# A hybrid decoder trunk: first sums of squares on TensorE, and a gate's reciprocal as exp(-ln)

## The chip, the cores and the metric

The kernel runs on one core of one Trainium2 chip. The metric is device microseconds of one launch, the median of several runs. Four compute engines work beside each other, each through its own queue of instructions in order: TensorE (PE; its weight loads are shown apart as PEld), VectorE (DVE), ScalarE (ACT) and GpSimd (POOL). SyncE (SP) only issues transfers here. An instruction waits at the head of its queue until the engines and transfers that it depends on have signalled, and everything behind it on that engine waits too.

## The reference, cut to what matters

Two layers, 512 tokens, 1024 features, all in float32. Each layer normalises its input, multiplies by one wide matrix, runs three groups of heads, and then an MLP:

```python
def rmsnorm(x, g):
    y = x * lax.rsqrt(jnp.mean(x * x, axis=-1, keepdims=True) + EPS)
    return y * g

h = rmsnorm(x, g_mix[l])
(cq, ckv, kr, aq, ak, av, qi, ki, wi, rq, rk, rv, rg) = jnp.split(h @ w_in[l], split_at, axis=-1)
...                      # three groups of heads: latent, sparse (top 128 keys), retention
ret = head_groupnorm(ret, g_ret[l])
o_c = jax.nn.silu(rg) * ret
x = x + jnp.concatenate([o_a, o_b, o_c], axis=-1) @ w_out[l]
hf = rmsnorm(x, g_mlp[l])
x = x + jnp.square(jax.nn.relu(hf @ w_ff1[l])) @ w_ff2[l]
```

`silu(rg)` is rg / (1 + exp(-rg)).

## The kernel before, in words

Activations stand with features on the 128 partitions and the 512 tokens along the free dimension, so the input is eight tiles `x[0]` to `x[7]` of 128x512. Every float32 product is made of three: a value is split into a rounded part (`hi`, `wh`) and the rest (`lo`, `wl`), and `mm3` adds hi·hi, hi·lo and lo·hi. A weight tile of 128 output columns (`win_tile(n)`) is one transfer into a buffer `wr`, two halves rounded by ACT or POOL into `wh` (L187, L189), the rests `wl` by DVE or POOL (L209, L211), and 24 matmuls into one PSUM bank `mm`. The rings are short: four buffers each for `wr`, `wh` and `wl`, three banks each for `mm` and `sc`.

The normalisation is taken out of the product: the matmuls read the bare x times the gain (`make_u`, u), and the factor 1/rms of each token multiplies the result when it leaves PSUM (`scaled`, by `rb`, which holds the factor in every partition; `rtok` holds it with tokens on partitions). So the first products can start before the factor is known, but nothing leaves PSUM until it is.

The factor of the first layer is made at the start: eight squares of x (L618 on POOL, L621 on ACT), seven adds into one tile `ss` (L624 on DVE), four matmuls of `ss` with a column of ones (`stats`, which put 128 tokens on partitions each), logarithm, exponential and one Newton step on 128x4 numbers (`rstd`), and four transposes that spread the result (`bcast`). The letters in `SQP` give the engine of each square: a is ACT, p is POOL.

The first products are, in order, tile 0 (keys; through `rope`), tiles 1 and 7 and 2 as the string `ORDER` lists them (`qi0 rg0 qi1`), and then `tk`, the token tiles, which are 96 matmuls of 328 columns. `rope` needs a transfer that swaps rows, two products with a table (one on POOL, one on DVE) and an add on DVE. After `tk` come the index scores (`sc` matmuls, relu on ACT, weighted sums on DVE), and from there on DVE finds the top 128 keys by rounds of MAX8 and MATCH_REPLACE8, which are set between everything else.

The gate is `rg_tile`, twice per layer: the tile leaves PSUM scaled, DVE clamps and negates it (L846), ACT takes the exponential (L847), POOL adds 1 (L848), DVE takes the reciprocal (L851), POOL multiplies (L852). The result is read much later, by `ret_done`.

What order the instructions take on each engine is settled when the program is built: a list scheduler places them by the order in which the code issues them, their dependencies, and the priorities in `PRI` (through `hp`); `tc.issue_after` holds an instruction back behind another. On the chip the order is fixed. So a change in one place can move instructions in others.

## Time and profile before

| | |
|---|---|
| runs | 1391.5, 1395.73 and 1395.9 us; median 1395.73 |
| the profiled execution's own time | 1398.68 us |
| its span | 1396.9 us |
| PE busy | 1326.8 us, 95% |
| DVE busy | 1103.2 us, 79% |
| ACT busy | 666.2 us, 48% |
| POOL busy | 331.6 us, 24% |
| granted clock of TensorE, mean | 0.976 |

A share of busy time is a mean over stages. How it is read: the span begins with some 40 us in which the first products wait for inputs; then comes a stretch up to about 330 us in which PE and DVE are both nearly full, then the MLP of the first layer in which PE has no gap, and the same again for the second layer. L numbers are lines of the kernel before. A row of a timeline gives the start, how long the engine was busy, the engine, the line, what is written and read, and in brackets how long the engine stood idle before it and what ended that. A granted clock of 1.00 is TensorE's upper level (2.4 GHz) and 0.50 its lower one (1.2 GHz).

### The profile page before, as it was taken

Reading aid. Unit: us, or ns where it says so; the run is one execution under the profiler, and the core shown is the slowest. Engines: PE = TensorE matmul, PEld = TensorE weight load, DVE = VectorE, ACT = ScalarE, POOL = GpSimd, SP = SyncE. Lnnn points to the kernel's source line nnn. Section 1 sums busy time; section 2 is a strip of 40 time slices with the busy share of each in tenths; the row PEclk is TensorE's granted clock in tenths of the full one; section 3 lists DMA queues with packets and bytes.
Section 4 is the critical chain, followed back from the end, with each engine's and each line's share of the span. In section 5 each row is a group of like instructions: output and inputs, shape, how many; then the busy total and the mean of one; then the engine's idle time right before and its main releaser. Section 6 shows DMA issues by size and latency. Waiting matters only on the chain. (4 is left out here: it accounts for less than half of the span.)

```text
span 1396.9 us, 20211 instructions
## 1 busy us (share of the span) xinstructions
PE 1326.8 (95%) x7304; PEld 1102.9 (79%) x7304; DVE 1103.2 (79%) x1843; ACT 666.2 (48%) x1179; POOL 331.6 (24%) x337
## 2 busy tenths in 40 slices
PE   7889988989999999999999999898999999999997
PEld 5767775757788888899988777566778888888997
DVE  6789998887677767788658999878767776777875
ACT  3343443676344344455535345357844444445652
POOL 4446752424100000000034666334240000000000
PEclk9999999999999999999999999999999999999998
DMA  6457522302355554556546671231035555554652
GB/s 218 99 162 183 157 64 70 113 16 63 123 192 171 183 174 154 180 180 215 178 143 188 192 181 52 77 100 46 16 121 163 164 179 178 161 180 151 209 184 78
DMA packets 75780, 197.56 MB, mean 141 GB/s; under 512 B 8960, under 2 KB 13792, under 8 KB 75680
## 3 DMA queue, kind: packets, MB, share of 16 engines
q1 hardware_dynamic: 74528, 195.22, 45.6%
q8 instruction: 58, 0.95, 0.3%
q10 hardware_dynamic: 1152, 1.05, 0.2%
q14 instruction: 42, 0.34, 0.1%
HBM read 155.68 MB, written 20.97 MB: 126 GB/s over the span
## 5 line engine op out<-in xcount | busy, mean ns | idle before, releaser
L141 PE MATMUL mm<-u,wh 128*128 128x512 f32 (+1 forms) x1776 | 561.5, 396 | 1.6 <-DVE u L284 1.2
L141 PEld LDWEIGHTS mm<-u,wh 128*128 128x128 f32 x1776 | 332.7, 190 | 77.4 <-DVE u L284 2.6
L141 PE MATMUL mm<-u,wl 128*128 128x512 f32 (+1 forms) x888 | 351.0, 395 | 3.9 <-DVE wl L209 3.9
L187 ACT ACTIVATE wh<-wr 128x512 fp32r<-128x512 f32 (+2 forms) x247 | 149.8, 611 | 315.8 <-PE mm L141 197.3
L209 DVE TENSOR_TENSOR wl<-wr,wh 128x512 fp32r<-128x512 f32 (+2 forms) x208 | 153.5, 739 | 89.6 <-ACT wh L187 87.3
L211 POOL TENSOR_TENSOR wl<-wr,wh 128x512 fp32r<-128x512 f32 (+2 forms) x80 | 104.7, 1309 | 443.3 <-ACT wh L187 423.7
L141 PEld LDWEIGHTS mm<-u,wl 128*128 128x128 f32 x888 | 168.8, 190 | 43.4 <-DVE wl L209 4.8
L489 DVE TENSOR_TENSOR u<-wr,u 128x1024 fp32r<-128x1024 f32 x54 | 65.8, 1221 | 25.1 <-ACT u L488 24.7
L141 PE MATMUL o<-p,v 128*128 128x512 f32 (+2 forms) x316 | 83.4, 370 | 1.8 <-POOL p L138 1.3
L488 ACT ACTIVATE u<-wr 128x1024 fp32r<-128x1024 f32 x54 | 57.1, 1058 | 53.3 <-PE o L502 14.0
L431 DVE TENSOR_TENSOR sm<-wr 128x512 f32<-128x512 f32 x64 | 44.5, 695 | 36.3 <-DMA wr<-in_wff 36.3
L502 PEld LDWEIGHTS sc<-g,v 128*128 128x128 f32 x576 | 70.3, 188 | 2.9
L502 PE MATMUL sc<-g,v 128*128 128x256 f32 x576 | 71.0, 277 | 0.0
L141 PEld LDWEIGHTS o<-p,v 128*128 128x128 f32 x316 | 52.4, 198 | 12.8 <-DVE p L138 4.1
L419 DVE SCALAR_TENSOR_TENSOR g<-mm,g 128x512 f32<-128x512 f32 x64 | 44.1, 688 | 23.0 <-PE mm L141 22.8
L138 DVE TENSOR_TENSOR p<-pe,p 128x512 fp32r<-128x512 f32 (+2 forms) x78 | 46.5, 623 | 12.0 <-POOL p L189 9.9
L189 POOL TENSOR_SCALAR p<-pe 128x512 fp32r<-128x512 f32 (+1 forms) x46 | 35.1, 767 | 74.2 <-ACT pe L1082 72.6
L735 DVE MATCH_REPLACE8 g<-m,g 128x512 f32<-128x512 f32 (+2 forms) x96 | 51.4, 539 | 0.0
L734 DVE MAX8 m<-g 128x8 f32<-128x256 f32 (+2 forms) x96 | 50.3, 547 | 0.2
L435 ACT ACTIVATE v<-wr 128x1024 fp32r<-128x1024 f32 x32 | 34.1, 1066 | 33.3 <-DVE wr L433 33.1
L189 POOL TENSOR_SCALAR wh<-wr 128x512 fp32r<-128x512 f32 (+3 forms) x41 | 29.8, 726 | 82.9 <-PE mm L141 57.6
L141 PE MATMUL sc<-u,qk 97*128 97x512 f32 (+5 forms) x192 | 46.7, 358 | 2.4 <-ACT pe L1082 2.4
(299 smaller groups left out, 2742.0 us busy)
## 6 DMA issues: line engine op xcount, KB each, us to landing
wr<-in_wff SPq DMA_DIRECT2D x160, 512.0 KB
wr<-in_win SPq DMA_DIRECT2D x37, 512.0 KB
ws<-sm SPq DMA_DIRECT2D x32, 512.0 KB
wr<-ws SPq DMA_DIRECT2D x32, 512.0 KB
tab<-in_tabs SPq DMA_DIRECT2D x20, 512.0 KB
wr<-in_wout SPq DMA_DIRECT2D x16, 512.0 KB
p<-p SPq DMA_DIRECT2D x40, 128.0 KB
wr<-in_wuq SPq DMA_DIRECT2D x12, 384.0 KB
```

Source lines behind the costliest of these rows:

```text
L138: (nc.vector if eng == "v" else nc.gpsimd).tensor_tensor(out, a, b, op=op)
L141: return nc.tensor.matmul(out, lhsT, rhs, start=start, stop=stop)
L187: nc.scalar.activation(out, src, AF.Copy)
L189: nc.gpsimd.tensor_scalar(out, src, 1.0, 1.0, op0=ALU.mult, op1=ALU.mult)
L209: nc.vector.tensor_sub(lo, rc, R(hi))
L211: nc.gpsimd.tensor_sub(lo, rc, R(hi))
L431: nc.vector.tensor_add(sm[:, h], w[0], w[1])
L488: nc.scalar.activation(wh, t, AF.Copy)
L489: nc.vector.tensor_sub(wl, t, R(wh))
L502: nc.tensor.matmul(outs[m][0], a[:, m * P : m * P + P], b, start=i == 0 and outs[m][1] and n == 0, stop=i == KP - 1 and n == 2, skip_group ...
L734: nc.vector.max(m8, accs[j])
L735: nc.vector.match_replace(out=accs[j], in_to_replace=m8, in_values=accs[j], imm_value=GONE)
```

## The change

In the first layer the tile `ss` and its seven adds are gone. Each square has a tile of its own; six are made by ACT and two (x[2] and x[5]) by DVE, none by POOL, and each is issued right behind the rounding of its x tile. TensorE adds them: behind the three matmuls of each x tile in tile 0 it multiplies the four blocks of the square with the column of ones, adding up all eight tiles in one PSUM bank (`sums`). The weights of tile 1 are prepared ahead of the Newton step, and two `after` hold the step behind the last split of those weights.

In the gate, POOL has nothing left to do. ACT takes exp, then ln(1 + e), then exp of minus that, which is a first value y of 1/(1 + e); DVE improves it by one Newton step and multiplies, with three SCALAR_TENSOR_TENSOR instructions.

```diff
-SQP = 'aapapapp'
+SQ = 'aavaavaa'
...
-            copy_fr(hi, rc, H0[n] if n < len(H0) else mode["hi"][n % len(mode["hi"])])
+            ins = copy_fr(hi, rc, H0[n] if n < len(H0) else mode["hi"][n % len(mode["hi"])])
+            if ins.ins.engine == order["uh"].ins.engine:
+                order["wh"] = ins
             if (L0[n] if n < len(L0) else mode["lo"][n % len(mode["lo"])]) == "v":
-                nc.vector.tensor_sub(lo, rc, R(hi))
+                order["wl"] = nc.vector.tensor_sub(lo, rc, R(hi))
...
-            u = [make_u(x[k], gcol(G0 + G_MIX + k)) for k in range(KD)]
-            ss = S("ss", 1)
+            u, squares = [], []
             for k in range(KD):
-                s = g_() if k else ss
-                if SQP[k] == "p":
-                    nc.gpsimd.tensor_mul(s, x[k], x[k])
+                u.append(make_u(x[k], gcol(G0 + G_MIX + k)))
+                s = g_()
+                squares.append(s)
+                if SQ[k] == "v":
+                    nc.vector.tensor_mul(s, x[k], x[k])
                 else:
-                    with after("uh"):
-                        nc.scalar.activation(s, x[k], AF.Square)
-                if k:
-                    with after("ul"):
-                        nc.vector.tensor_add(ss, ss, s)
+                    nc.scalar.activation(s, x[k], AF.Square)
+            ch, out, sums = wsplit(first, 1024, 2), mm_ps(), sc_ps()
+            for k in range(KD):
+                h, w = ch[k // 4]
+                js = slice(k % 4 * P, k % 4 * P + P)
+                mm3(out, h[:, js], w[:, js], *u[k], k == 0, k == KD - 1)
+                for b in range(NB):
+                    nc.tensor.matmul(sums[:, b : b + 1], squares[k][:, b * P : (b + 1) * P], ones,
+                                     start=k + b == 0, stop=k == KD - 1, skip_group_check=True)
+            begun[0] = out
+            ready[1] = wchunk(win[l, 1], 1024)
             rtok = tiny(4, "rtok", 2)
-            nc.vector.tensor_copy(rtok, stats(ss, 1024))
+            with hp("st"), after("wh"), after("wl"):
+                y = rstd(sums[:, :NB], 1024)
+            nc.vector.tensor_copy(rtok, y)
...
                 nc.scalar.activation(e, e, AF.Exp)
-                nc.gpsimd.tensor_scalar(e, e, 1.0, 1.0, op0=ALU.mult, op1=ALU.add)
-                for b in range(0, T, T // 4 if OPT_R else T):
-                    b = slice(b, b + (T // 4 if OPT_R else T))
-                    nc.vector.reciprocal(e[:, b], e[:, b])
-                nc.gpsimd.tensor_mul(sg, sg, e)
+                y = g_()
+                nc.scalar.activation(y, e, AF.Ln, bias=ones)
+                nc.scalar.activation(y, y, AF.Exp, scale=-1.0)
+                nc.vector.scalar_tensor_tensor(e, e, 1.0, y, op0=ALU.add, op1=ALU.mult)
+                nc.vector.scalar_tensor_tensor(y, e, 2.0, y, op0=ALU.subtract, op1=ALU.mult)
+                nc.vector.scalar_tensor_tensor(sg, sg, -1.0, y, op0=ALU.mult, op1=ALU.mult)
```

Lines move by one from L190 on and by about fifteen from L660 on: the adds at L624 are gone, the new matmuls with the ones are L629, the gate's L846 is L860 and its new instructions are L861 to L867.

On TensorE, the sums of the kernel before stand once, behind the first matmul of the third tile (`mm_336`, tile 7, the gate); `sc_194` is the bank of the sums, u and `wh`, `wl` are activations and weights:

```order
L141 MATMUL mm_286<-u_167,wh_282 128x512 x2
L141 MATMUL mm_286<-u_167,wl_283 128x512
L141 MATMUL mm_336<-u_146,wh_328 128x512
L141 MATMUL sc_194<-ones,ss_170 128x1 x4
L141 MATMUL mm_336<-u_146,wh_328 128x512
L141 MATMUL mm_336<-u_146,wl_329 128x512
```

In the changed kernel they stand inside tile 0 (`mm_194`), four behind each of the eight tiles of x; the bank is `sc_195`, `g_149` to `g_184` are the squares:

```order
L141 MATMUL mm_194<-u_146,wh_186 128x512 x2
L141 MATMUL mm_194<-u_146,wl_187 128x512
L629 MATMUL sc_195<-ones,g_149 128x1 x4
L141 MATMUL mm_194<-u_151,wh_186 128x512
L629 MATMUL sc_195<-ones,g_154 128x1 x4
L141 MATMUL mm_194<-u_151,wh_186 128x512
L141 MATMUL mm_194<-u_151,wl_187 128x512
L141 MATMUL mm_194<-u_156,wh_186 128x512
L629 MATMUL sc_195<-ones,g_159 128x1 x4
```

So four matmuls of one column between whole tiles became thirty-two inside the first, and the four transposes that spread the factor moved from tile 7 up to tile 1.

On POOL, behind the weights of the first tiles, the kernel before has the first product of `rope` (`p_249`, of tile 0, with the table `tab_251`) behind the copy of a weight of the token tiles (`wh_478`):

```order
L189 TENSOR_SCALAR wh_375<-wr_369 128x512
L211 TENSOR_TENSOR wl_376<-wr_369,wh_375 128x512
L211 TENSOR_TENSOR wl_433<-wr_426,wh_432 128x328
L189 TENSOR_SCALAR wh_478<-wr_476 128x328
L138 TENSOR_TENSOR p_249<-p_249,tab_251 128x512
```

In the changed kernel the same product (`p_280`) stands ahead of both token weights:

```order
L189 TENSOR_SCALAR wh_399<-wr_393 128x512
L212 TENSOR_TENSOR wl_400<-wr_393,wh_399 128x512
L138 TENSOR_TENSOR p_280<-p_280,tab_282 128x512
L212 TENSOR_TENSOR wl_457<-wr_450,wh_456 128x328
L138 TENSOR_TENSOR p_332<-p_332,tab_305 128x512
L189 TENSOR_SCALAR wh_502<-wr_500 128x328
```

The product of `rope` thus moved ahead of two weights and no longer stands behind a copy into a ring buffer.

On DVE, at the first gate, the kernel before has the reciprocal (of `g_363`) behind a `rope` of tile 2 (`p_404`) and ahead of two weights of the tiles that follow the token tiles (`wl_691`, `wl_786`):

```order
L209 TENSOR_TENSOR wl_529<-wr_526,wh_528 128x328
L846 TENSOR_SCALAR g_363<-g_361 128x512
L138 TENSOR_TENSOR p_404<-p_404 128x512
L232 TENSOR_TENSOR g_412<-p_404,g_411 128x512
L851 RECIPROCAL g_363<-g_363 128x512
L209 TENSOR_TENSOR wl_691<-wr_688,wh_690 128x512
L209 TENSOR_TENSOR wl_786<-wr_783,wh_785 128x512
```

In the changed kernel the gate's three instructions stand ahead of that `rope` (`p_428`), with one weight of the token tiles (`wl_507`) between the clamp and them:

```order
L860 TENSOR_SCALAR g_384<-g_382 128x512
L210 TENSOR_TENSOR wl_507<-wr_500,wh_506 128x328
L865 SCALAR_TENSOR_TENSOR g_384<-g_384,g_387 128x512
L866 SCALAR_TENSOR_TENSOR g_387<-g_384,g_387 128x512
L867 SCALAR_TENSOR_TENSOR g_382<-g_382,g_387 128x512
L210 TENSOR_TENSOR wl_553<-wr_550,wh_552 128x328
L138 TENSOR_TENSOR p_428<-p_428,tab_305 128x512
L138 TENSOR_TENSOR p_428<-p_428 128x512
L233 TENSOR_TENSOR g_436<-p_428,g_435 128x512
L210 TENSOR_TENSOR wl_715<-wr_712,wh_714 128x512
```

The gate moved ahead of the `rope` of tile 2, and the weight `wl_715` (as `wl_691` before) now has that `rope` in front of it instead of the reciprocal.

## Rows read from the trace of the kernel before

**Rows 1.** Windows: us, busy us (instructions) by engine, granted clock, DMA share, GB/s.

```profile
26.50:30.00 3.50, 3.46 (x12) 3.20 (x13) 0.82 (x5) 0.47 (x2) 0.00 (x0) 0.50 0.43 150
...
60.00:64.00 4.00, 3.98 (x11) 2.98 (x11) 4.00 (x8) 0.00 (x0) 3.33 (x3) 0.57 0.85 178
...
100.00:200.00 100.00, 94.53 (x396) 72.14 (x394) 94.67 (x205) 41.76 (x82) 62.11 (x59) 0.95 0.52 139
...
400.00:460.00 60.00, 60.00 (x333) 51.54 (x332) 44.60 (x72) 25.27 (x40) 0.00 (x0) 1.00 0.55 176
```

**Rows 2.** Timeline of PE: start us, us, what, [idle before and its releaser].

```profile
6.13 0.93 PE L141 MATMUL mm<-u,wh 128*128 128x512 f32 x2
...
17.18 0.50 PE L141 MATMUL mm<-u,wl 128*128 128x512 f32 x1 [1.92 <-DVE wl L209]
...
22.41 0.40 PE L141 MATMUL mm<-u,wh 128*128 128x512 f32 x1
...
26.54 1.83 PE L141 MATMUL sc<-ones,ss 128*128 128x1 f32 x8 [3.74 <-DVE ss L624]
...
28.24 0.77 PE L141 MATMUL mm<-u,wh 128*128 128x512 f32 x1
...
33.18 0.39 PE L141 MATMUL mm<-u,wl 128*128 128x512 f32 x1
...
41.58 0.40 PE L141 MATMUL mm<-u,wl 128*128 128x512 f32 x1
```

**Rows 3.** Timeline of PE, one-column sums between layers, and the instruction after.

```profile
694.00 1.02 PE L362 MATMUL sc<-ones,g 128*128 128x1 f32 x8
...
694.88 0.72 PE L502 MATMUL sc<-v,qk 128*128 128x256 f32 x4
```

**Rows 4.** By line and form, before: the adds of the squares.

```profile
L624 DVE TENSOR_TENSOR ss<-ss,g 128x512 f32<-128x512 f32 x7 | 8.5, 1208 | 0.3
```

**Rows 5.** Timeline of ACT, first logarithm of the sums.

```profile
28.42 0.26 ACT L244 ACTIVATE tiny<-sc,epst 128x4 f32<-128x4 f32 x1 [8.21 <-PE sc L141]
```

**Rows 6.** Timeline of DVE: copy of the factor, later waits.

```profile
29.54 0.17 DVE L626 COPY rtok<-tiny 128x4 f32<-128x4 f32 x1
...
59.28 2.30 DVE L209 TENSOR_TENSOR wl<-wr,wh 128x512 fp32r<-128x512 f32 x2
...
113.29 0.69 DVE L644 TENSOR_TENSOR p<-mm,g 128x512 f32<-128x512 f32 x1 [1.82 <-PE mm L141]
```

**Rows 7.** Timeline of PE, later waits of layer 1.

```profile
53.79 0.42 PE L141 MATMUL mm<-wl,u 128*128 128x328 f32 x1 [0.64 <-DVE wl L209]
...
59.95 0.71 PE L141 MATMUL mm<-u,wl 128*128 128x512 f32 x1 [1.98 <-DVE wl L209]
...
65.62 0.38 PE L141 MATMUL sc<-g,v 96*128 96x256 f32 x1 [1.64 <-ACT g L722]
...
214.89 1.19 PE L141 MATMUL mm<-x,wh 128*128 128x512 f32 x2 [4.93 <-DVE g L976]
```

**Rows 8.** Timeline of PE, the same place in layer 2.

```profile
890.60 1.19 PE L141 MATMUL mm<-x,wh 128*128 128x512 f32 x2 [4.38 <-DVE g L976]
```

**Rows 9.** Timeline of POOL, rope waiting behind a weight copy.

```profile
41.90 0.47 POOL L189 TENSOR_SCALAR wh<-wr 128x328 fp32r<-128x328 f32 x1 [4.21 <-issue]
```

**Rows 10.** Timeline of ACT, rounding of the first activations.

```profile
8.57 3.43 ACT L283 ACTIVATE u<-x,gn 128x512 fp32r<-128x512 f32 x5 [0.26 <-DMA x<-in_xT]
```

**Rows 11.** Lines 847, 851 and 1043: count: duration min/median/max, first and last start us.

```profile
L847 ACT ACTIVATE g<-g x4: 632/632/633, 54.1 to 797.0; 128x512 f32<-128x512 f32 x4
...
L851 DVE RECIPROCAL g<-g x4: 3340/3352/3353, 56.0 to 799.4; 128x512 f32<-128x512 f32 x4
...
L1043 DVE SCALAR_TENSOR_TENSOR g<-g,g x8: 679/688/1787, 261.8 to 1004.0; 128x512 f32<-128x512 f32 x8
```

**Rows 12.** Timeline of DVE, the last reciprocal.

```profile
799.42 3.35 DVE L851 RECIPROCAL g<-g 128x512 f32<-128x512 f32 x1 [0.55 <-POOL g L848]
```

**Rows 13.** Timeline of POOL beside it.

```profile
799.35 1.29 POOL L211 TENSOR_TENSOR wl<-wr,wh 128x512 fp32r<-128x512 f32 x1
```

More of the change, by code (lines that the diff above doesn't have):

```diff
@@ L186, in copy_fr @@
         if eng == "a":
-            nc.scalar.activation(out, src, AF.Copy)
-        elif eng == "p":
-            nc.gpsimd.tensor_scalar(out, src, 1.0, 1.0, op0=ALU.mult, op1=ALU.mult)
-        else:
-            nc.vector.tensor_copy(out, src)
+            return nc.scalar.activation(out, src, AF.Copy)
+        if eng == "p":
+            return nc.gpsimd.tensor_scalar(out, src, 1.0, 1.0, op0=ALU.mult, op1=ALU.mult)
+        return nc.vector.tensor_copy(out, src)
     def wchunk(src, width, parts=2):
@@ L634, in trunk_kernel, with win_tile @@
             nxt.finish(xp, late, sums)
-        def win_tile(n, raw=None):
+        def win_tile(n):
+            if l == 0 and n in begun:
+                return begun[n]
             if n in begun:
@@ L639, in win_tile @@
                 return product(ch, k8, u, late, out)
-            return gemm(win[l, n], k8, u, raw)
+            if n in ready:
+                return product(ready[n], k8, u)
+            return gemm(win[l, n], k8, u)
         def scaled(ps, z):
@@ L645, in scaled @@
             return z
-        z = rope(scaled(win_tile(0, first if l == 0 else None), zz_()), table(T_M), mixed)
+        z = rope(scaled(win_tile(0), zz_()), table(T_M), mixed)
         kmh, kml, kmd = S("km", 3, None, FR), S("km", 3, None, FR), S("km", 3, None, FR)
```

2 lines of the change are left out of this document (1 added, 1 removed).

## The prediction

> **What bounds the kernel now.** I read the busy shares first: PE is busy 95% of the span, so a change pays only where PE stands still or runs at its lower clock, and costs wherever it puts work on PE. Then the windows, to see where that is: in the MLP of the first layer PE fills 60.00 of 60.00 us at a granted clock of 1.00, so whatever is won ahead of it is carried through it whole; from 100 to 200 us PE and DVE are both nearly full (94.53 and 94.67 of 100) [rows 1]. Then PE's timeline of the first 60 us, because the first part of the change lies there. The reader is to see four things in it [rows 2]. The first product starts at 6.13. The second stops 1.92 us for a weight of DVE. The third does one matmul at 22.41 and then PE stands 3.74 us, until DVE has added the last square; only then, at 26.54, come the sums. And behind that wait the clock is 0.50, the lower level [rows 1]; ahead of it the 22 matmuls from 17.18 to 22.41 took 0.238 us each, which is the upper level's pace. The last matmul of the fourth product starts at 41.58. Last I read who holds whom later: waits of 0.64, 1.98 and 1.64 us between 53 and 66 us, and one of 4.93 us at 215 us, with its twin of 4.38 us in the second layer at 891 us [rows 7, 8].
>
> **The rate of PE.** From 33.18 to 41.58 PE does 36 matmuls of 512 columns without a gap: 8.40 / 36 = 0.2333 us each [rows 2]. A one-column float32 matmul runs as two passes, each with a weight load of its own: the four of the sums show as eight records [rows 2], and between layers eight passes take 694.88 - 694.00 = 0.88 us, 0.11 us each, at the upper clock [rows 3]. At the lower clock eight take 28.24 - 26.54 = 1.70 us, 0.2125 each [rows 2]. The Trainium skill (TensorE: Matmul & The Clock Gate, section "Wait — 56ns, not 53.3ns?") gives about 25 ns as the least start-to-start time of a narrow matmul; by it the 64 new passes would be 1.6 us, an estimate, and the sum below would be 5.4 us better. The row is four times that, since here each pass brings new weights, and the row decides.
>
> **The start, part by part.** Before, four products are 96 x 0.2333 = 22.40 us of matmuls, and from 6.13 to the end of the fourth (41.58 + 0.23 = 41.81) pass 35.68 us: 13.28 us are gaps, half clock, and the sums themselves. After, PE has in the same four products 22.40 us of matmuls, 64 passes x 0.11 = 7.04 us, four transposes (none is in my rows at the upper clock; I bound each by a whole 512-column matmul, 0.93 together, and take 0.9; from below by the four passes' 0.44), and about 0.4 us until the clock has risen. Sum 30.74, so the fourth product ends 35.68 - 30.74 = 4.9 us earlier, if nothing starves PE.
> What could starve it: first ACT, which now makes six squares between the roundings of x. Its last five roundings take 3.43 us from 8.57, to 12.00 [rows 10]. An ACT pass over 128x512 takes 0.63 [rows 11]; two squares fit into the time before 8.57, where ACT waited for x, the other four push the end to 12.00 + 4 x 0.63 = 14.5 us. PE needs that last square when it has done 22 matmuls and 56 passes, at 6.13 + 0.4 + 5.1 + 6.2 = 17.8. So PE is the later one by 3 us, and ACT costs nothing. DVE loses the seven adds, 8.5 us in all [rows 4], and gets two squares, about 1.4 us at the 0.69 us of its two-input operations [rows 11]; its weight that held PE 1.92 us at 17.18 stands ahead of the adds now. The added waits: the logarithm and the Newton step. From the logarithm at 28.42 [rows 5] to the end of the copy at 29.71 [rows 6] they take 1.29 us; the transposes stand behind two matmuls of the first and six of the second product, 8 x 0.2333 = 1.87 us, so they are covered. Without that cover the cost would be 1.3 us once. Queued behind the step on DVE are only weights of the third product, which PE reaches 5 us later.
>
> **The waits at 53 to 66 us.** The wait of 1.98 us at 59.95 is for a weight that DVE began at 59.28 [rows 6, 7], right behind the reciprocal of 3.35 us [rows 11]; behind it the clock was 0.57 for the four microseconds to 64 [rows 1], which costs 4 x 0.43 = 1.7 us more. After, two things in front of that weight are gone. The reciprocal is replaced by three instructions that stand earlier, ahead of a rope that is there in both. And the rope of the first product no longer waits on POOL behind a weight copy, which stood idle 4.21 us until 41.90 [rows 9], when PE let go of a buffer at 41.81: its POOL product now comes ahead of both token weights, so a stretch of DVE's work moves from behind 42 us to before 35 us, into time that was free. I take the 1.98 and the 1.7 as gone, 3.7 us, and of the 0.64 at 53.79, also a weight on DVE, another 0.6. Between 0 and 4.3 is possible: below nothing would need DVE later than before, and it has 8.5 us less to do. What is late next is the wait of 1.64 us at 65.62: ACT's relu stands behind the splits of the token tiles, which need DVE's means of them. Nothing of that chain goes away; I take 0, with 1.64 as the other end. DVE then waits for PE again at 113.29, for 1.82 us [rows 6]; so PE's lead is DVE's lead from there on, and both carry it into the full stretch.
>
> **The gate, four times.** Removed per gate: 3.35 us of DVE, two POOL operations. Added: two ACT passes of 0.63 us (ACT is busy 48%) and three SCALAR_TENSOR_TENSOR. The nearest row of these is line 1043, same operation and size: least 0.679, median 0.688, longest 1.787, against a reciprocal that is 3.340 to 3.353 all four times [rows 11]. So DVE gets between 3.35 - 3 x 0.688 = 1.29 us back and 3 x 1.787 - 3.35 = 2.0 us more per gate. The spread is POOL's: while the last reciprocal ran (799.42, 3.35 us [rows 12]), POOL's operation from 799.35 took 1.29 us beside it [rows 13], and neither was longer; two-input operations beside POOL are. The Trainium skill (SBUF — State Buffer, section "Who interferes with whom") has the rule: a DVE instruction with two SBUF inputs and a GpSimd instruction that reads SBUF exclude each other for a whole instruction, one with a single input does not. The reciprocal has one, each of the three new ones two. The trace agrees; by the median the four gates are -5.2 us of DVE, by the rule at its worst +8.0.
> Of that only gates 2 and 4 can reach PE, since they stand ahead of the waits of 4.93 and 4.38 us for DVE [rows 7, 8]; 1 and 3 come where DVE has time. The added wait is DVE's for ACT's chain of three passes, 1.9 us: behind it in DVE's queue stand weights of the token tiles at gate 1, PE's products at gates 2 and 4, where other DVE work is set between. I take the gates at 0, between -2.6 and +4.0.
>
> **Sum.** -4.9 (start) - 4.3 (waits at 53 to 64) + 0 (65.62) + 0 (gates) = -9.2 us. Against the profiled execution's own 1398.68 us (span 1396.9 and 1.8 around it) that is 1389.5; that execution was 3.0 us above the median of the runs, so the time is 1395.73 - 9.2 = 1386.5 us.
>
> **Rivals.**
> 1. PE's clock falls in the first product. More than half of it will be one-column passes, and no row shows so many together; the eight at 694 us do not lower the clock, but they stand between full matmuls. At the lower level the first product takes 24 x 0.467 + 64 x 0.2125 = 24.8 us in place of 12.6, so the start is 7.3 us slower than before instead of 4.9 faster. Against it the 4.3 of the later waits: 1398.7, and 1403.0 if those stay, slower in both cases. It decides if the granted clock is 0.5 for more than about two thirds of the stretch from 7 to 20 us. For it: the clock does fall at the start when PE has little to do. Against: PE has no gap there now.
> 2. PE's lead is spent in the full stretch. The order of DVE's top-128 rounds, products and weights is new, and PE would wait there longer, up to the 4.9 us of the start: 1391 to 1394. For it: DVE at 94.67 of 100 us. Against: DVE waits for PE at 113 and has less to do.
> 3. The three new DVE operations run beside POOL, the rule above. At their longest in gates 2 and 4 they add 4.0 us ahead of the two waits: 1390.5. For it: POOL is busy 62 of the 100 us around gate 2 [rows 1]. Against: half of the eight at line 1043 take 0.688 or less.
> 4. The gates' DVE time and the wait at 65.62 both come back: 1386.5 - 2.6 - 1.6 = 1382.3.
>
> **How the numbers follow.** Forecast 55%, rival 1 7%, rival 2 13%, rival 3 12%, rival 4 13%. Time 1386.5. The low end takes rival 4 whole and one more microsecond that POOL leaves DVE alone, 1381; the high end is a start worth 1.4 (passes at half as much again as the row, 3.5 us more) with one microsecond of the waits gone, 1393.5; rival 1 and the slow part of rival 2 lie outside. A measurement of this kernel tells about 0.3%, 4.2 us, from no change. Faster than 1391.5: forecast, rival 4, two thirds of rival 3, a third of rival 2, 0.80. Slower than 1399.9: half of rival 1 and what of the new order I can't see, 0.06. The rest, 0.14, within 0.3%.
>
> **What would show it.** The first product ends near 19.6 us and the fourth near 37, at a clock of 1.00 from 7 us on; passes of 0.11 us; no wait for the sums. The wait in front of the tile behind the token tiles is gone, with its half clock. The reciprocal's three successors take 0.69 each, or up to 1.79 beside POOL. PE's waits near 210 and 880 us are about as long as before. Wrong would be: a clock of 0.5 in the first product, PE idle in it for a square, or a first-layer MLP that begins less than 5 us earlier than before.

## The result, and the profile after

The changed kernel took 1379.51 us (median of 4 executions, 1376.64 to 1383.08) against 1395.82 (4 executions) of the kernel before beside it: ratio 0.9885, 95% interval 0.986 to 0.9911. Two later measurements gave 0.9865 (0.9836 to 0.9895) and 0.9891 (0.9852 to 0.993). So it is 15 to 19 us faster; 9.2 were forecast, and the time lies 1.5 us below the low end of the range. The direction was right and the sum too small.

The profiled execution after has a span of 1374.9 us. It is the quickest of its four and the one of before was 3 us above its median, so these two traces lie 22 us apart, some 6 more than the medians. The windows that answer to [rows 1]:

```profile
26.50:30.00 3.50, 3.50 (x18) 2.88 (x17) 1.57 (x2) 0.48 (x1) 2.10 (x2) 1.00 0.69 178
60.00:64.00 4.00, 4.00 (x21) 3.15 (x20) 3.86 (x8) 1.93 (x7) 1.43 (x1) 1.00 0.51 150
100.00:200.00 100.00, 93.38 (x411) 72.73 (x411) 96.63 (x208) 46.62 (x88) 65.05 (x62) 0.97 0.47 125
400.00:460.00 60.00, 60.00 (x335) 52.52 (x335) 44.79 (x73) 25.66 (x41) 0.00 (x0) 1.00 0.56 176
```

In this execution both stretches of half clock are gone. PE's timeline of the start, beside [rows 2]:

```profile
6.38 0.81 PE L141 MATMUL mm<-u,wh 128*128 128x512 f32 x2
...
7.26 0.95 PE L629 MATMUL sc<-ones,g 128*128 128x1 f32 x8
8.06 0.49 PE L141 MATMUL mm<-u,wh 128*128 128x512 f32 x1
...
19.27 0.62 PE L141 MATMUL mm<-u,wh 128*128 128x512 f32 x2
...
20.66 0.60 PE L266 MATMUL sc<-cft,rtok 128*128 128x128 f32 x4
...
27.04 0.39 PE L141 MATMUL mm<-u,wl 128*128 128x512 f32 x1
...
35.88 0.39 PE L141 MATMUL mm<-u,wl 128*128 128x512 f32 x1
36.11 0.31 PE L141 MATMUL mm<-wh,u 128*128 128x328 f32 x1
```

No wait for sums is left, eight passes take 8.06 - 7.26 = 0.80 us, and the four products last 36.11 - 6.38 = 29.73 us (30.74 forecast). The first product, from 6.38 to 19.27, takes 12.89 us; less 24 matmuls of 0.2267 that leaves 7.45 us for the 64 passes, 0.116 each, since the first matmul behind a group of passes is longer too. One thing was not in the forecast: from 27.04 to 35.88 there are 39 matmuls of 512 columns, 8.84 / 39 = 0.2267 us each, where before had 0.2333 [rows 2].

Later waits of PE, beside [rows 7, 8]:

```profile
58.48 0.50 PE L141 MATMUL mm<-u,wl 128*128 128x512 f32 x1 [0.68 <-DVE wl L210]
...
72.26 0.50 PE L141 MATMUL sc<-g,v 96*128 96x512 f32 x1 [2.26 <-ACT g L736]
...
88.84 0.50 PE L141 MATMUL sc<-qk,qk 128*128 128x512 f32 x1 [2.09 <-DMA qk<-g]
...
193.58 1.08 PE L141 MATMUL mm<-g,wh 128*128 128x512 f32 x2 [2.01 <-DVE qk L233]
...
868.11 1.19 PE L141 MATMUL mm<-x,wh 128*128 128x512 f32 x2 [4.49 <-DVE g L991]
```

The 1.98 at 59.95 is 0.68, the 1.64 at 65.62 is gone, the 4.93 at 214.89 has become 2.01 for another tile, and its twin in layer 2 stands (4.49). The row at 72.26 is the successor of one of before:

```profile
84.44 0.80 PE L141 MATMUL sc<-g,v 96*128 96x512 f32 x1 [3.39 <-ACT g L722]
```

The three new instructions on DVE, at the first gate and at the second:

```profile
41.27 0.69 DVE L865 SCALAR_TENSOR_TENSOR g<-g,g 128x512 f32<-128x512 f32 x1 [1.44 <-ACT g L864]
41.99 1.27 DVE L866 SCALAR_TENSOR_TENSOR g<-g,g 128x512 f32<-128x512 f32 x1
43.30 0.69 DVE L867 SCALAR_TENSOR_TENSOR g<-g,g 128x512 f32<-128x512 f32 x1
```

```profile
107.77 1.17 DVE L865 SCALAR_TENSOR_TENSOR g<-g,g 128x512 f32<-128x512 f32 x1
...
109.47 1.55 DVE L866 SCALAR_TENSOR_TENSOR g<-g,g 128x512 f32<-128x512 f32 x1
...
111.55 0.68 DVE L867 SCALAR_TENSOR_TENSOR g<-g,g 128x512 f32<-128x512 f32 x1
```

Where the 22 us lie, stage by stage, worked out from the starts of the same PE instructions in each trace (us). The first and the fourth column are the two traces above; the others are of experiments below ("again" and "third": the same kernel once more).

```
                                           before  before  new start  after   after   after  after,
stage                                              again                      again   third  old layout
first matmul to the token tiles' end        51.22   47.61   51.41      45.21   55.62   46.86   45.13
to the first retention score (L141 qk,qk)   45.48   45.47   37.31      37.25   36.91   36.48   37.01
to the transposes of the q factor (L266)    98.64   98.66   99.67      93.98   94.44   98.38   94.50
to the MLP's first transposes              166.38  166.35  166.78     162.94  163.84  169.18  163.20
first MLP                                  326.15  325.82  324.29     323.67  324.29  324.66  327.76
second layer up to its MLP                 353.92  354.19  356.13     357.81  355.11  356.95  349.21
second MLP                                 323.16  324.85  321.76     321.51  321.16  320.86  325.25
```

The stretch behind the token tiles is the largest single gain, 8.2 us, and the only large one that every trace shows: 45.5 us in both traces of the kernel before, 36.5 to 37.3 in the three of the changed kernel. The first stage is not so steady: it is 47.61 and 51.22 us in the kernel before, 45.21 to 55.62 in the changed one. The window of the stretch before, then after, then in another execution of the changed kernel (columns as in [rows 1]):

```profile
57.35:102.83 45.48, 37.08 (x149) 28.60 (x147) 41.38 (x73) 19.42 (x47) 18.02 (x17) 0.92 0.53 145
```

```profile
51.59:88.84 37.25, 32.23 (x142) 24.96 (x140) 36.87 (x64) 19.51 (x48) 17.20 (x16) 1.00 0.54 156
```

```profile
61.39:98.30 36.91, 33.67 (x142) 26.37 (x140) 36.47 (x63) 19.68 (x47) 16.77 (x16) 0.95 0.56 160
```

PE stands still 45.48 - 37.08 = 8.40 us before and 5.02 after, and the mean clock rises from 0.92 to 1.00. But in the third window the clock is 0.95 and the stretch no longer, so the clock does not set its length after the change. DVE does: it is busy 36.87 of 37.25 us. Of the 8.2 us, 41.38 - 36.87 = 4.5 are work that DVE no longer has in this stretch (nine instructions fewer), and 4.10 - 0.38 = 3.7 are time in which it stood still. Most of that was one wait of the kernel before, for ACT's relu of the scores:

```profile
73.12 2.25 DVE L727 SCALAR_TENSOR_TENSOR g<-g,wtok,g 128x256 f32<-128x256 f32 x4 [3.06 <-ACT g L722]
```

No wait of that size is left after; DVE now comes to this stretch with part of its work done.

### The profile page after: what moved, and what is told of

It reads as the page before. It is cut to its first block, busy times and chain, and to the rows that moved or that the text cites. A ratio compares the mean times of both kernels' runs of the same rounds, so it can differ in the third digit from the quotient of the medians.

```text
span 1374.9 us, 20315 instructions
## 1 busy us (share of the span) xinstructions
PE 1317.4 (96%) x7358; PEld 1112.0 (81%) x7360; DVE 1091.4 (79%) x1846; ACT 670.6 (49%) x1189; POOL 323.3 (24%) x325
## 4 chain that ended last, share of the span: by engine, by line
PE 71%; DVE 16%; ACT 4%; issue 4%; DMA 3%; POOL 1%; POOLq 0%; SPq 0%; DVEq 0%; ACTq 0%
PE mm L141 40%; PE sc L503 11%; PE sc L141 5%; PE mm L503 5%; PE o L503 5%; PE o L141 3%; DVE p L138 2%; DVE g L749 2%; DVE wl L210 2%; DVE m L748 1%; DMA wr<-in_win 1%; DVE g L741 1%; DMA wr<-in_wff 1%; DVE g L233 1%; PE sc L363 1%
## 5 line engine op out<-in xcount | busy, mean ns | idle before, releaser
L141 PE MATMUL mm<-u,wh 128*128 128x512 f32 (+1 forms) x1776 | 552.0, 390 | 0.0
L141 PE MATMUL mm<-u,wl 128*128 128x512 f32 (+1 forms) x888 | 345.6, 389 | 0.7 <-DVE wl L210 0.7
L189 POOL TENSOR_SCALAR p<-pe 128x512 fp32r<-128x512 f32 (+1 forms) x46 | 38.9, 850 | 74.2 <-ACT pe L1097 71.0
L138 DVE TENSOR_TENSOR p<-pe,p 128x256 fp32r<-128x256 f32 (+2 forms) x78 | 48.6, 648 | 9.4 <-POOL p L189 7.0
L503 PE MATMUL o<-g,v 128*128 128x256 f32 x384 | 50.5, 281 | 0.0
```

The source lines that it names most:

```text
L138: (nc.vector if eng == "v" else nc.gpsimd).tensor_tensor(out, a, b, op=op)
L141: return nc.tensor.matmul(out, lhsT, rhs, start=start, stop=stop)
L503: nc.tensor.matmul(outs[m][0], a[:, m * P : m * P + P], b, start=i == 0 and outs[m][1] and n == 0, stop=i == KP - 1 and n == 2, skip_group ...
```

## The experiments

**Both kernels again, and each part alone.** The new start with the old gate ends its gate with these lines, as before:

```
-                y = g_()
-                nc.scalar.activation(y, e, AF.Ln, bias=ones)
...
+                nc.gpsimd.tensor_scalar(e, e, 1.0, 1.0, op0=ALU.mult, op1=ALU.add)
...
+                    nc.vector.reciprocal(e[:, b], e[:, b])
+                nc.gpsimd.tensor_mul(sg, sg, e)
```

The new gate on the old start is the reverse of it in the kernel before.

> The kernel before, unchanged, for two questions. First the pace: in the profile of before three 512-column matmuls take 0.700 us everywhere in the MLP, in the profile of after 0.681, both at a granted clock of 1.00; in the MLPs alone that is 5.9 us (365.8 against 363.2 and 378.5 against 375.3). Theory 'pace belongs to the run': this trace may show 0.681 or 0.700 here, and start_only and gate_only either as well. Theory 'pace belongs to the change': 0.700 here, 0.681 in after_again. Second the spread: a ratio to before of 1.000 within 0.003.

> The changed kernel, unchanged. Ratio near 0.9885 (-16 us) if the first four runs were typical. If the pace belongs to the run, its MLP of the first layer takes 363 to 366 us like any other; if to the change, 363. The layers outside the MLP: about 22 us shorter in the first, about 5 us longer in the second, if these two differences come from the order of the instructions and not from one execution.

> The new start (sums of squares on TensorE), the gate as before (exp, add on POOL, DVE reciprocal, product on POOL). Theory 'start': the first 100 us give nearly all, -12 to -16 us, and the order behind them follows. Theory 'gate': DVE time of the gates gives what my sum lacked, so the start alone is the -9 of my prediction, 1386 to 1388. The wait of PE in front of the tile behind the token tiles stays away under both, since the adds are gone; its half clock too.

> The start as before, the new gate (exp, ln, exp, three DVE instructions). Theory 'start': within 2 us of before; the waits of 3.7 us for the last add and of 2 us at 60 us stay. Theory 'gate': -5 to -8 us, from the stretch between 57 and 330 us. Theory 'lock' (DVE's two-input operations beside POOL): slower by up to 4 us.

Measured against 1398.74 us: before again 0.9998 (0.9975 to 1.002), after again 0.9865, new start 0.9913 (0.9885 to 0.994), new gate 1.0025 (1.0001 to 1.0048). The start is worth some 12 us alone, the gate alone costs 3.5 (barely clear of nothing), yet both together gain 15 to 19: the gate gains only on top of the start. That last step is 3 to 7 us by the medians, though the intervals of the new start and of the changed kernel overlap.

Three things came with these traces. First, the long wait for the sums and the half clock behind it [rows 1, 2] belong to one execution of the kernel before. In the other the wait is 1.12 us, the eight passes run at the upper level, and the fourth product ends at 37.97 instead of 41.81:

```profile
25.48 1.02 PE L141 MATMUL sc<-ones,ss 128*128 128x1 f32 x8 [1.12 <-DVE ss L624]
```

Second, 0.2267 us per 512-column matmul stands in every trace with the new start so far and 0.2333 in every one with the old. The two programs differ in where their tiles lie: the old start takes `ss`, `rtok` and `tiny` from the pool ahead of the weights' tiles, so that `wh` begins at byte 99072 of a partition, with the new start at 96704. Third, the six executions of the changed kernel lie in two groups, 1375.5 to 1378.6 and 1383.7 to 1384.9 us. The profiled one is of the second group; windows of its start, granted clock in the third column from the right:

```profile
7.00:14.00 7.00, 6.54 (x38) 5.45 (x36) 6.20 (x7) 6.88 (x12) 3.08 (x4) 0.83 1.03 394
14.00:20.00 6.00, 6.00 (x25) 5.61 (x25) 3.16 (x4) 0.79 (x2) 1.35 (x1) 0.50 0.62 244
20.00:26.00 6.00, 6.00 (x23) 5.23 (x22) 0.00 (x0) 0.00 (x0) 0.00 (x0) 0.50 0.00 0
26.00:32.00 6.00, 6.00 (x18) 4.93 (x19) 1.66 (x7) 1.85 (x5) 0.00 (x0) 0.50 0.00 0
```

The clock is at its lower level from 14 to 32 us, and the fourth product ends at 46.43 instead of 36.11. That is rival 1, in a part of the executions. It is not the only thing that makes an execution long: the profiled one of the third measurement (after third, 1386.15 us) has its fourth product done at 37.45 and is longer later, at a mean clock of 0.94 where the trace above has 0.98:

```profile
187.41:356.59 169.18, 156.73 (x755) 116.85 (x756) 133.97 (x211) 97.02 (x194) 66.26 (x69) 0.94 0.23 74
```

**Place alone, in both directions.** Instructions and their order are those of the parent kernel on every engine; only the order in which tiles are first taken changes.

```
             (changed kernel)
+            S("ss", 1), tiny(4, "rtok", 2), tiny(4)
             ch, out, sums = wsplit(first, 1024, 2), mm_ps(), sc_ps()
             (kernel before)
+            S("wh", WB, None, FR), S("wl", WB, None, FR)
             ss = S("ss", 1)
```

> The changed kernel with the same instructions in the same order on every engine; only three unused tiles (ss, rtok, tiny) are taken from the pool ahead of the weights' tiles, so that these lie 2368 bytes higher, where they lay before the change (byte 99072 of a partition in place of 96704). Theory A, the pace of TensorE's 512-column products hangs on where the weights lie in SBUF against the activations they meet (same place modulo 2048 bytes, or 320 bytes on): three of them take 0.70 us again in place of 0.681, and the kernel is 5 to 12 us slower than the changed one, about 1387 to 1393. Theory B, the quicker pace comes from the order of the start or from what other engines do: 0.681 us, and no change in time (1376 to 1383).

> The kernel before with the same instructions in the same order; only the pool hands out the weights' tiles first, so that they lie at byte 96704 as in the changed kernel. Theory A (place in SBUF): three 512-column products take 0.681 us in place of 0.700 and the kernel is 5 to 12 us faster than before, about 1384 to 1391. Theory B (order or neighbours): 0.700 us, and as long as before within 2 us (1394 to 1398).

Two rows of each, first the changed kernel with the old places (39 matmuls of 512 columns apart), then the kernel before with the new ones (33 apart):

```profile
27.64 0.39 PE L141 MATMUL mm<-u,wl 128*128 128x512 f32 x1
...
36.74 0.40 PE L141 MATMUL mm<-u,wl 128*128 128x512 f32 x1
```

```profile
29.68 0.39 PE L141 MATMUL mm<-u,wl 128*128 128x512 f32 x1
...
37.17 0.39 PE L141 MATMUL mm<-u,wl 128*128 128x512 f32 x1
```

That is 9.10 / 39 = 0.2333 us with the old places and 7.49 / 33 = 0.2270 with the new: the pace goes with the places, not with the start.

In time: the changed kernel with the old places 1384.26 us, 0.9908 (0.9874 to 0.9943), some 4 us slower than the changed kernel's three measurements (mean 0.988), though the intervals overlap; its MLPs are 4.1 and 3.7 us longer (table). The kernel before with the new places: 1394.0, 0.9992 (0.9972 to 1.0013); its MLPs are 1.8 and 1.5 us shorter than in the trace of before, and of the 5 to 12 us that theory A asked for no more than 4 can be there. The paces moved as theory A says; the price in time was put too high. One reason is in the same traces: at the new places the 576 products of `g` and `v` in each MLP take 0.1178 us, where the first trace of before has 0.1135, which takes back 2.5 us.

**The pace by itself.** TensorE alone, 36 matmuls at each of 33 places:

> Not the kernel but TensorE alone: 36 products of 128x128 weights by 512 columns at each of 33 places of the weights, 64 bytes apart from the activations' place modulo 2048 bytes on; first with the other engines idle, then with VectorE and ScalarE copying beside it. Its output is a copy of a product, not the trunk's. Theory A: the pace steps between about 0.227 and 0.233 us with the place, quick at 0 and slow at 320 bytes (the sixth place), with the engines idle too. Theory A2, the place matters only when other engines use SBUF: 33 equal paces in the first half, steps in the second. Theory B: equal in both.

Each place is closed by two 256-column products into `mk`. The timeline of the first places, with the other engines idle:

```profile
29.54 0.40 PE L98 MATMUL ps<-u,wt 128*128 128x512 f32 x1
...
37.72 0.40 PE L104 MATMUL mk<-u,wt 128*128 128x256 f32 x2
37.95 0.39 PE L98 MATMUL ps<-u,wt 128*128 128x512 f32 x1
...
46.35 0.40 PE L104 MATMUL mk<-u,wt 128*128 128x256 f32 x2
46.58 0.39 PE L98 MATMUL ps<-u,wt 128*128 128x512 f32 x1
...
54.95 0.39 PE L104 MATMUL mk<-u,wt 128*128 128x256 f32 x2
55.18 0.40 PE L98 MATMUL ps<-u,wt 128*128 128x512 f32 x1
...
63.44 0.39 PE L104 MATMUL mk<-u,wt 128*128 128x256 f32 x2
```

From first to marker, 36 matmuls take 8.18, 8.40, 8.37 and 8.26 us: 0.2272, 0.2333, 0.2325 and 0.2294 us each, for weights 0, 64, 128 and 192 bytes further than the columns. The four values repeat every 256 bytes through both halves of the run (each within 0.0005), idle neighbours or not. In the kernel before, the weights lie 320 bytes on from `u` modulo 2048, that is 64 modulo 256: 0.2333. In the changed one they lie at 0: 0.2267. Theory A holds for 512 columns, and A2 and B fall.

**256 columns.** The same as the MLP's second half feeds it:

> TensorE alone again, as the MLP's second half feeds it: 128x128 weights by 256 columns, three to an output, at 17 places of the weights 64 bytes apart, first with the other engines idle, then with VectorE and ScalarE copying. Its output is a copy of a product, not the trunk's. Theory A: four paces that repeat every 256 bytes, as with 512 columns, quickest at 0, and the slow one near 0.118. Rival: one pace whatever the place.

The rows between two markers hold 144 matmuls; markers of the first places:

```profile
53.78 1.07 PE L106 MATMUL mk<-u,wt 128*128 128x512 f32 x4
...
71.97 0.63 PE L106 MATMUL mk<-u,wt 128*128 128x512 f32 x2
...
88.76 0.62 PE L106 MATMUL mk<-u,wt 128*128 128x512 f32 x2
...
106.32 0.64 PE L106 MATMUL mk<-u,wt 128*128 128x512 f32 x2
```

Less the markers' own two matmuls (0.46 us) that is 16.33 us between the second and the third, 0.1134 each, and 17.10 to the fourth, 0.1188. All four, at 0, 64, 128 and 192 bytes: 0.1199, 0.1133, 0.1188, 0.1178, every 256 bytes again. So the quick place is another one than for 512 columns: the theory is right on four paces and wrong on which is quickest.

**Both rules tried in the kernel.** Unused bytes ahead of `p` and `qk`, 192 and 128 in the first, 128 and 192 in the second:

```
             bcast(rtok, rb)
+            tiny(48, "pad_p", 1)        (second: 32)
...
             wtoks.append(wtok)
+            if l == 0:
+                tiny(32, "pad_qk", 1)   (second: 48)
```

> The changed kernel, the same instructions in the same order; 192 unused bytes ahead of the tiles p and 128 ahead of qk, so that p, km, v and qk too lie at the place modulo 256 bytes at which u, x, g and the weights lie (192). The sweep showed 0.227 us for 512-column products whose two operands share that place and 0.233 where the weights lie 64 bytes on. Theory A, this holds for the other products as well: the MLP's 256-column products of g and v (0.1178 us each in the changed kernel) fall to about 0.113 and those of p and v too, and the kernel is 4 to 9 us faster than the changed one (1371 to 1377). Rival: the 256-column products change between 0.1133 and 0.1178 with the place unchanged (both occur within one execution), so they are paced by something else, and the time stays (1378 to 1385).

> The changed kernel, same instructions in the same order; 128 unused bytes ahead of p (p, km and v then lie at 128 modulo 256 in place of 0) and 192 ahead of qk (192 in place of 128). By the sweeps, the 256-column products with weights in u and columns in v (64 apart in place of 192) should go from 0.1178 to 0.1133 us (528 of them, -2.4 us), and the 512-column products of qk and the weights from 0.233 to 0.227 (192, -1.2 us); g and v come 192 apart, where 0.1178 is what the changed kernel has now. Theory A: 2 to 4 us faster than the changed kernel, 0.982 to 0.985 of before, and 6 to 8 us faster than aligned, whose 256-column products took 0.1200. Rival, the paces in the kernel are set otherwise: u with v stays at 0.1178, time as the changed kernel's (0.9865 to 0.9885).

Measured: the first 1382.61 us, 0.9914 (0.9881 to 0.9947), no gain; the second 1376.04, 0.9841 (0.9808 to 0.9875). The products of `u` with `v` show it. A group of 24 in the changed kernel, with the row behind it, then in the first and in the second layout:

```profile
603.45 2.99 PE L503 MATMUL mm<-v,u 128*128 128x256 f32 x24
606.28 0.99 PE L503 MATMUL sc<-v,u 128*128 128x256 f32 x7
```

```profile
606.53 3.04 PE L503 MATMUL mm<-v,u 128*128 128x256 f32 x24
609.41 0.76 PE L503 MATMUL sc<-v,u 128*128 128x256 f32 x5
```

```profile
611.72 2.90 PE L503 MATMUL mm<-v,u 128*128 128x256 f32 x24
614.46 0.73 PE L503 MATMUL sc<-v,u 128*128 128x256 f32 x5
```

2.83, 2.88 and 2.74 us for 24: 0.1179, 0.1200 and 0.1142, near what the sweep has for 192, 0 and 64 bytes (0.1178, 0.1199, 0.1133). The products of `g` and `v` follow the rule in both layouts (0.1200 at 0 bytes, 0.1178 at 192), but in the changed kernel they take 0.1178 where the sweep has 0.1133 for their 64. The kernel before, at 64 as well, shows 0.1135 in both MLPs of its first trace, and 0.1137 in the first and 0.1175 in the second MLP of the other. So for these products the place is not all; what else sets them stays open.

> tuned_layout once more, beside the changed kernel. If the layout is worth 2 to 4 us as the paces say (u with v 0.1178 to 0.1133 in 528 products, qk with the weights): 0.982 to 0.985, and 2 to 4 us below after_third. If the first run was chance: as after_third.

> The changed kernel once more, with nothing altered, beside tuned_again on the same chip: 0.9865 to 0.9885 of before, as in its two earlier measurements.

Side by side 1378.0 (0.9882, 0.9846 to 0.9919) and 1378.85 us (0.9891): 0.9 us apart. The pace came out the same as the first time (0.1142), the time did not: the spread between executions (1372.6 to 1387.4) hides two microseconds. It had the lowest median both times, by an amount that these runs do not settle.

**The clock at the start.** The passes put into the second product, with `issue_after` behind each step of it:

```
-                mm3(out, h[:, js], w[:, js], *u[k], k == 0, k == KD - 1)
...
+                order["p1"] = mm3(out, h[:, js], w[:, js], *u[k], k == 0, k == KD - 1)
+                with after("p1"):
+                    for b in range(NB):
```

> The changed kernel with the 64 one-column passes taken out of the first product and put between the steps of the second, four matmuls after each step. Theory C, the passes in the first product are what lets TensorE's clock fall to 0.50 in part of the executions: the clock stays 1.00 through the first four products, the executions stay together near the quicker group of the changed kernel (1375 to 1378), and the 4th product ends at 35.5 to 37 us. Rival, the first product itself (waits for x and its copies) lets it fall: the clock is at 0.50 in 14 to 30 us as often as in the changed kernel, and the times spread to 1384. Against both: the statistics come 5 to 6 us later, and if that is not covered, the token tiles' copies and the first scaled product wait for them, 3 to 6 us slower.

Measured 1393.9 us, 0.9992 (0.9969 to 1.0014), by the ratios 14 to 18 us slower than the changed kernel, a miss for both theories. The window of its first product:

```profile
7.00:14.00 7.00, 5.11 (x19) 2.98 (x18) 7.00 (x9) 6.48 (x12) 3.74 (x3) 1.00 1.04 402
```

PE stands still 1.89 of these 7 us, while DVE and the DMA queues are full: without the passes the first product waits for x and its copies, and the passes had used part of that time. The first product ends at 15.72 us without them and at 19.27 with them, so the 64 passes, 7.45 us of PE's work, put its end back by 3.5. The fourth product ends at 40.34, the clock is 1.00 up to 56 us, and the statistics are 10 us later (transposes at 30.31 in place of 20.66). The stretch behind the token tiles takes 42.20 us instead of 37.25, so it is long again when the statistics come late. The rest of the loss was not taken apart; the order on the other engines moved as well.

With half the passes:

```
-                s = g_()
+                s = g_(FR)
...
-                    nc.tensor.matmul(sums[:, b : b + 1], squares[k][:, b * P : (b + 1) * P], ones,
+                    nc.tensor.matmul(sums[:, 2 * b : 2 * b + 2], squares[k][:, b * P : (b + 1) * P], onefr,
```

> The changed kernel with the squares and the column of ones rounded to fp32r, two equal columns of ones: 32 passes in the first product in place of 64, in the same places; all tiles 32 bytes on together. Theory C, the passes cost TensorE's time and let its clock fall: about 0.1 us each, 32 fewer, less what the first product waits for x anyway: 4th product's end 1 to 3 us earlier, the clock at 1.00 from 7 to 30 us more often, median 3 to 6 us below the changed kernel (0.983 to 0.985). Rival, the first product waits for x and its copies (as sums_second showed, which had gaps there without the passes) and the clock falls for that: no gain, 0.9865 to 0.9885, and the clock falls as often.

Measured 1380.13 us, 0.9861 (0.9823 to 0.9898), executions from 1369.17 to 1387.92; the interval holds the ranges of both. In the profiled one the clock is 0.80 from 7 to 14 and 0.50 from 14 to 20 us and the fourth product ends at 40.08, so half the passes do not prevent the fall; how often it comes, one trace does not tell. Eleven traces here have the passes in the first product. From 14 to 20 us the clock is 1.00 in four of them, 0.72 in three and 0.50 in four. In the last four PE stood still for 0.07 to 0.79 us between 7 and 14, but standing still alone does not bring the fall: without the passes PE stood 1.89 us and the clock stayed at 1.00. The kernel before falls there too (0.89 from 14 to 20 in its second trace, 0.80 with the new places), and in both the fourth product ended earlier (37.97 and 37.40) than in the first trace (41.81), whose clock fell later, behind the wait for the sums. What starts the fall was not found.

**The gate by layers, and on the old start at the new places.**

```
+                if l == 0:        (second: l == 1)
...                                 the new gate
+                else:
...                                 the old gate
```

> New start; the new gate in layer 1 alone, the old one (reciprocal) in layer 2. New start with the old gate in both was 0.9913 of before, with the new gate in both 0.9865 to 0.9885. Theory G1, the gate's gain is made in layer 1, where the earlier statistics let VectorE work ahead, and layer 2's gates cost 1 to 2 us (in the traces the stretch from the kv factor to the second MLP's first product is that much longer with the new gate): 1 to 3 us faster than the changed kernel, 0.984 to 0.988. Rival G2, both layers share it: 0.989 to 0.990. Rival G3, the gate gains nothing and the 6 us are chance between executions: 0.991.

> The counterpart: new start; old gate in layer 1, new gate in layer 2 alone. G1: as new start with the old gate or 1 to 2 us slower, 0.991 to 0.993. G2: 0.989 to 0.990. G3: 0.991.

> Old start, new gate, and the weights' tiles at the changed kernel's place (byte 96704): gate_only's instructions in gate_only's order, other addresses. Without the new gate this place gave 0.9992 of before. Theory P, the gate is worth 3 to 6 us on the old start as well, and gate_only lost it to the pace of the 256-column products (0.1133 to 0.1178, +4.4 us over both MLPs): 0.9955 to 0.998. Theory S, the gate pays only behind early statistics: 0.999 to 1.002.

Measured: layer 1 alone 0.9888 (0.9864 to 0.9911), layer 2 alone 0.9911 (0.9878 to 0.9944), the old start at the new places 0.9992 (0.9974 to 1.0009), the same as without the new gate. So the gate gains nothing on the old start, at either place: theory S. Between layers the medians point to layer 1 (0.9888 against 0.9911, the value of the new start with the old gate), but the intervals overlap. A wait tells more. With the new start and the old gate:

```profile
208.70 1.19 PE L141 MATMUL mm<-x,wh 128*128 128x512 f32 x2 [5.11 <-DVE g L990]
```

With the old start and the new gate (old start, new places):

```profile
216.28 1.19 PE L141 MATMUL mm<-x,wh 128*128 128x512 f32 x2 [4.39 <-DVE g L978]
```

Only with both does it go: 2.01 to 2.05 us in the changed kernel's traces and in gate_l1, 5.11 in gate_l2. In layer 2 the wait is 4.4 to 4.5 in all of them. From the first retention score to the MLP, the two traces with the new start and the old gate in layer 1 take 266.5 and 263.1 us (new start, gate_l2). With the new gate there they take 256.9, 258.3 and 259.8 (after, after again, gate_l1), and 267.6 in after third, whose clock was low in this stretch.

## Why the prediction was too small

**The start came out right in the profiled pair, in part by luck.** The fourth product was to end at 6.13 + 30.74 = 36.9 us and ends at 36.11; there is no wait for the sums, and the statistics stand behind products that hide them. But the terms were off both ways: matmuls 96 x 0.2267 = 21.8 us (22.4 forecast), passes with what they lengthen 7.45 (7.04), transposes 21.02 - 20.66 = 0.36 (0.9), and nothing for a rise of the clock (0.4), which is 1.00 from 5 us on. And the 35.68 us of before, from which the gain of 4.9 was taken, hold only for that execution: from the first matmul to the fourth product's end pass 35.68 and 32.06 us in the two traces of the kernel before, and 29.73, 40.65 and 31.76 in the three of the changed one. What the start stage gains by itself these runs do not fix.

**The waits at 53 to 66 us were undersized: the first step that failed.** It took 4.3 us and set the wait at 65.62 to 0, "nothing of that chain goes away". The stretch up to the first retention score gave 8.2, with either gate (new start: 37.31). The 1.64 went, the one at 84.44 fell from 3.39 to 2.26, and DVE, which sets the length of the stretch, had 4.5 us less to do in it and stood still 3.7 us less. The 1.7 us for half clock in this step are not shown: a changed kernel with the clock at 0.95 there took no longer. The step looked at PE's waits singly; what moved was DVE as a whole. Rival 4 had the wait at 65.62 come back, and its 1382.3 us was the nearest of all. Rival 2 did not come: the stretch behind, to the q factor's transposes, is shorter and not longer.

**The gate was put at 0 and is worth some 3 to 7 us, only behind the new start: the second step.** The bounds (-2.6 to +4.0) were for each engine's time in the old order. That time is not where the gain lies: DVE takes 0.69 + 1.27 + 0.69 = 2.65 us at the first gate against 3.35 [rows 11], but 1.17 + 1.55 + 0.68 = 3.40 at the second, which stands ahead of the wait that shrank. The Trainium skill (SBUF — State Buffer, section "Who interferes with whom") has the rule by which two-input operations of DVE and a GpSimd instruction that reads SBUF exclude each other; the trace agrees in part: one of three is longer at the first gate and two at the second, 1.17 to 1.55 us and not 1.79, and the third is not. So rival 3 had the mechanism and the wrong sign of the sum. The wait of 4.93 [rows 7] lost 2.9 us with both changes; either alone leaves 4.4 to 5.1. That both gate and statistics had to leave DVE's queue ahead of it is the likely reason; it is argued here and not shown. Adding two terms worked out singly missed the gain.

**The pace of PE was taken as given: the third step.** Every term used 0.2333 us [rows 2]. The change took one tile out of the pool's first places, the weights moved 2368 bytes, and the pace became 0.2267: 2.5 and 1.7 us less in the MLPs against before, 4.1 and 3.7 us against the same kernel at the old places. No view of the profile of before shows places in SBUF; it was shown by the sweep and by the two kernels that differ from their parents in nothing else. The Trainium skill (TensorE: Matmul & The Clock Gate, section "Wait — 56ns, not 53.3ns?") has a fixed 2.5 ns per matmul beyond the columns' time, 215.7 ns for 512 columns; the runs here, with float32r products that each load weights, disagree: 226.9 to 233.3 ns by place. It also (SBUF — State Buffer, "Who interferes with whom") calls TensorE's reads of weights and of columns independent; that the pace hangs on the place of the one against the other speaks against that for these float32r products.

**What worked against it.** Rival 1, at 7%, is not an alternative but comes in some of the executions. Of the three profiled ones of the changed kernel one has a clock of 0.50 from 14 to 32 us, ends its fourth product 10 us later and is 8.2 us longer than the first; one has 0.72 from 14 to 20 and loses little by it. And the second layer up to its MLP is 1 to 4 us longer than before in these three traces, but 5 shorter in the same kernel at the old places; this was not settled.

So, by the means of the two traces of before and the three of the changed kernel (table), the stage of the start gains 0.2 us and not 4.9 (3.4 without the trace at the low clock); the stretch behind the token tiles 8.6 and not 4.3; the two stages from there to the MLP, with the first layer's gates, 4.1 and not 0; the MLPs, with the pace, 4.6 and not 0; and the second layer ahead of its MLP loses 2.6. That makes 15. The start's mean hangs on which executions were profiled, and the single terms are good to a few microseconds.

## What to carry to other kernels

Before costing a change, ask whether it alters which tiles a pool hands out first: the same instructions at other addresses moved PE's pace by up to 2.8% at 512 columns and 5.8% at 256, and a tile shifted by 64 bytes is a free experiment. Where a change relieves an engine that trails PE, cost the stretch by the engine that sets its length, not wait by wait, and cost two edits that shorten the same queue together. Profile more than one execution of a kernel whose first products wait for data, before the prediction too: here the clock and the waits of the first 40 us differ from one execution of the same kernel to the next.

## What the runs showed of the hardware

With TensorE alone, the pace of back-to-back float32r matmuls hangs on the weights' place less the columns' place modulo 256 bytes, in steps of 64 as measured: 0.2269, 0.2332, 0.2325, 0.2294 us with 512 columns and 0.1199, 0.1133, 0.1188, 0.1178 with 256, at a granted clock of 1.00, the same beside copies of VectorE and ScalarE. The quick place differs with the number of columns. In the kernels the 512-column products follow this; one kind of 256-column product showed two paces at one place. One-column float32 passes cost 0.10 us each in a group of eight at clock 1.00 (0.116 with the longer matmul behind the group) and 0.2125 at 0.50. Inside a first product that waits for its inputs, 64 of them put its end back by 3.5 us (15.72 to 19.27), where their own work is 7.45. The granted clock of the first products differs between executions of one kernel: 1.00, 0.72 and 0.50 from 14 to 20 us in three of the changed kernel.
